# A pace, an interleaving and a first load changed in a two-block transformer kernel

## The chip, the cores and the metric

The kernel runs on one core of one Trainium2 chip. The metric is device time in microseconds (us) of one execution. Three runs of the kernel before took 1598.66, 1603.24 and 1604.40 us.

The engines are named as in the profile: PE multiplies matrices (PEld loads its stationary operand beside the products), DVE (VectorE) and ACT (ScalarE) work elementwise, POOL is GpSimd, SP only issues transfers here.

## The reference

Two blocks run one after the other on 256 tokens of width 1024, in float32. The first has two gated feed-forward layers, a mixer and an embedding gate; the second an attention block and a layer of experts that are looked up by product keys. The parts that matter here, shortened:

```python
def swiglu(x, w_gate, w_up, w_down):
    return (jax.nn.silu(x @ w_gate) * (x @ w_up)) @ w_down

h = h + 0.5 * swiglu(rms_norm(h, ln_ffn1[i]), w1_gate[i], w1_up[i], w1_down[i])
...
def peer_ffn(h, w_query, sub_keys, expert_u, expert_v):
    q = jnp.einsum('bsd,dk->bsk', h, w_query).reshape(B, S, PEER_HEADS, 2, PEER_HALF)
    sc = jnp.einsum('bshpc,hpnc->bshpn', q, sub_keys)
    s1, i1 = lax.top_k(sc[..., 0, :], PEER_TOPK)
    s2, i2 = lax.top_k(sc[..., 1, :], PEER_TOPK)
    cand_s = (s1[..., :, None] + s2[..., None, :]).reshape(...)
    cand_i = (i1[..., :, None] * N_KEYS + i2[..., None, :]).reshape(...)
    top_s, sel = lax.top_k(cand_s, PEER_TOPK)
    idx = jnp.take_along_axis(cand_i, sel, axis=-1)
    gates = jax.nn.softmax(top_s, axis=-1)
    ...
        u = expert_u[ec]
        a = jax.nn.gelu(jnp.einsum('cd,chkd->chk', xc, u), approximate=False) * wc
        return jnp.einsum('chk,chkd->cd', a, expert_v[ec])
```

There are 128 x 128 experts, 8 heads, and 16 experts for each head and token.

## The kernel before

Every float32 product is done as three: an operand is split into a high part (ACT, line 288) and a low rest (DVE, line 289), and high x low, high x high and low x high are summed (lines 314 to 324). A weight tile comes by a transfer that SP issues into a `raw` buffer; ACT makes `wh` from it and DVE `wl`; then PE uses both.

**The start.** x is loaded in four pieces (`xload(c, j)`: chunk c of 128 tokens, half j of the width). `wraw1(k, h)` loads tile k of the first weights `w1t` in h pieces. 18 products of a zero tile `z` (line 720) come first on PE. `n1.part(c, j)` transposes a piece of x on PE (line 512) and splits it into `hH` and `hL` (lines 516, 519). `cut["n"]` says in how many pieces a weight tile is split by ACT and DVE. `tm_proj` takes tile k for chunk 0 as it comes and for chunk 1 four tiles later; its `parts` say behind which tile a further piece of x is transposed.

**The expert stage (`peer`).** Instead of gathering expert rows, the kernel computes all of them. `ublock(i)` multiplies the u rows of 128 experts (first index i) with all 256 tokens: 24 products of 128x256 (lines 322 to 324) into one of four `mm` banks; gelu goes into `G[:, i, :]`. The matrix of gates comes from `wgroup(g)`, four tokens at a time: for each token PE multiplies two one-hot matrices (`B`/`BL` with `O`, lines 1615, 1616; 8 products of 128x128 a group) into an `acc` bank. DVE makes the one-hots for two groups at once in four instructions (`onehots`, lines 1601 to 1604). What exists of G for these tokens is multiplied by the gates on DVE (line 1621); where G is still to come, ACT writes the gates into G (line 1623) and a later u-block multiplies its gelu with them (lines 1634, 1635). `slotT` holds the indices and gates that the one-hots are made from. It is filled per chunk of 128 tokens by `rowcol(c)`, eight `lookup(c, half, q)` (three DVE instructions each, lines 1566, 1568, 1569) and `gates(c)` (with three transposes on PE, line 1582). Groups 0 to 31 need chunk 0, groups 32 to 63 chunk 1. After the last u-block and group, the output stage multiplies G with the v rows of each i: `operands` splits `G[:, i]` into `aH` and `aL`, and 12 products of 128x512 follow (lines 318 to 320).

**The order.** All of this background work stands in a deque `bg` with a cost for each item. After every block `run(c)` adds credit c and takes items while the credit is above 0; c is `QC` = 1.2 in the 16 query steps and `UC` = 1.0 in the 127 u-blocks after the first. What is left in `bg` is done behind the last u-block (lines 1678, 1679). A scheduler then sets the order on each engine from this program order; it may pull an instruction forward whose operands are there. Each engine takes its row in order. The deque's items for the lookup and the groups are filled in chunk by chunk:

```python
        for c in range(2):
            bg.append((1.2, lambda c=c: rowcol(c)))
            for k in range(8):
                bg.append((0.9, lambda c=c, k=k: lookup(c, *divmod(k, 4))))
            bg.append((0.8, lambda c=c: gates(c)))
            for g in range(32 * c, 32 * c + 32):
                bg.append((1.25, lambda g=g: wgroup(g)))
```

Of the kernel before, what the change touches and what calls it, by code (L numbers as in the profile page):

```python
# [13 lines left out]
OP = mybir.AluOpType  # L14
# [6 lines left out]
NEG = -1e30  # L21
FT = 4
TAIL = (5, 5)
UC = 1.0
QC = 1.2
FILL = 1200
LATE = (2, 3, 4, 5, 6, 7, 8, 9, 9, 10, 11, 12)
# [4 lines left out]
FW = 3  # L32
PR = 2
WN = 18
G2 = (0,) * 8
OKIND = ("at", "mm")
FLAG = (4, 4)
# [160 lines left out]
def _build(tc, nc, A, out, stop=99, dbg=None):  # L198
    ctx = ExitStack()
    mm_, act, dve, pool = nc.tensor.matmul, nc.scalar, nc.vector, nc.gpsimd  # L200
# [52 lines left out]
    col = const.tile([128, NCOL], F32, name="col")  # L253
# [30 lines left out]
    def ins_of(i):  # L284
        return getattr(i, "ins", i)
# [17 lines left out]
    def wsplit(raw, n=1024, p=None, g=None):  # L303
        H, L = ((p or ws[t]).tile([128, 1024], F32R, tag=t, name=t)[:, :n] for t in ("wh", "wl"))
        if gate:
            g = gate.pop()
        m = n // cut["n"]
        for i in range(0, n, m):
            if g is not None:
                pool.tensor_copy(H[:, i:i + 1], g)  # L310
            split(raw[:, i:i + m], H[:, i:i + m], L[:, i:i + m])
        return H, L
# [384 lines left out]
    n1 = RawNorm(hA, lambda dt: K("ln_ffn1", dt))  # L697
    raw1 = {}

    def wraw1(k, h=1):  # L700
        raw1[k] = ws["raw"].tile([128, 1024], F32, tag="raw", name="raw")
        m = 1024 // h
        for i in range(0, 1024, m):
            nc.sync.dma_start(raw1[k][:, i:i + m], A["w1t"][k][:, i:i + m])

    wraw1(0, 2)
    wraw1(1)
    xload(1, 0)
    wraw1(2)
    xload(0, 1)  # L710
# [4 lines left out]
    with TP("warm") as p:  # L715
# [2 lines left out]
        ps = fill_bank((128, 256))  # L718
        for _ in range(WN):
            mm_(ps, z[:, 0:128], z, start=True, stop=True)  # L720
    dve.tensor_scalar(col[:, 0:48], col[:, 0:48], 32.0, None, op0=OP.mult)
    n1.part(0, 0)
    cut["n"] = 2
    with tc.issue_after(ins_of(n1.first_act)):
        first = {0: wsplit(raw1.pop(0))}
    cut["n"] = 1
    identb = mb[:, 0:128]
    maskb = mb[:, 128:256]
# [37 lines left out]
    modp = spare.enter_context(TP("modp", 2))  # L766
    with TP("ffw1", TLW[0], side="right") as pw1:
        ffn(n1, 1, extra(FT, range(M0), NF - 1), n2, pw1, first, before_tail=ple_proj, raws=raw1,
            parts={0: (1, 0), 1: (0, 1), 2: (1, 1)})
    dump("x1", xr)  # L770
    if stop <= 1:
        pstack.close(); big.close(); early.close()
# [682 lines left out]
    def peer():  # L1455
# [87 lines left out]
        def rowcol(c):  # L1543

            slots[c] = G[:, 112:115, 128:256]
            a, w, i, j = (spare16[:, 2 + n_ // 2, n_ % 2 * 128:n_ % 2 * 128 + 128] for n_ in range(4))
            s_ = G[:, 115, 128:256].bitcast(U32)
            sf = sel[c].rearrange("p h k -> p (h k)")
            dve.tensor_scalar(s_, sf, 3, None, op0=OP.logical_shift_right)
            dve.tensor_copy(a, s_)  # L1550
            dve.tensor_scalar(s_, sf, 7, None, op0=OP.bitwise_and)
            dve.tensor_copy(w, s_)
            dve.scalar_tensor_tensor(j, a, 9.0, w, op0=OP.is_ge, op1=OP.mult)
            dve.tensor_sub(w, w, j)
            dve.tensor_scalar(i, a, -1.0, 0.0, op0=OP.add, op1=OP.max)
            dve.tensor_add(i, i, j)
            dve.tensor_scalar(j, a, 1.0, 8.0, op0=OP.is_equal, op1=OP.mult)
            dve.tensor_add(j, j, w)
            ij[c] = [x_.rearrange("p (h k) -> p h k", h=8) for x_ in (i, j)]

        def lookup(c, half_, q):

            e4 = spare16[:, 0:2].rearrange("p h (k j) -> p h k j", j=16)
            sv = ij[c][half_][:, 2 * q:2 * q + 2]
            iv = idxf[c].rearrange("p (h two) k -> p h two k", two=2)[:, 2 * q:2 * q + 2, half_]
            dve.tensor_tensor(e4, sv.unsqueeze(3).to_broadcast([128, 2, 16, 16]),
                              iob[:, 0:16].unsqueeze(1).unsqueeze(1).to_broadcast([128, 2, 16, 16]), op=OP.is_equal)
            dve.tensor_tensor(e4, e4, iv.unsqueeze(2).to_broadcast([128, 2, 16, 16]), op=OP.mult)
            dve.tensor_reduce(slots[c][:, half_, q * 32:(q + 1) * 32].rearrange("p (h k) -> p h k", h=2), e4,
                              axis=AX.X, op=OP.add)  # L1570

        def gates(c):
            g = slots[c][:, 2].rearrange("p (h k) -> p h k", h=8)
            dve.tensor_sub(g, tops[c], tops[c][:, :, 0:1].to_broadcast([128, 8, 16]))
            act.activation(g, g, AF.Exp)
            sm = ps_.tile([128, 8], F32, tag="gs", name="gs")
            dve.reduce_sum(sm, g, axis=AX.X)
            dve.reciprocal(sm, sm)
            dve.tensor_tensor(g, g, sm.unsqueeze(2).to_broadcast([128, 8, 16]), op=OP.mult)
            ps = mm_bank((128, 3, 128))  # L1580
            for i in range(3):
                nc.tensor.transpose(ps[:, i], slots[c][:, i], ident)

            sT = slotT[:, :, c * 128:(c + 1) * 128]
            two = [128, 128, 2]
            for i in range(2):
                act.activation(sT[:, i], ps[:, i].unsqueeze(2).to_broadcast(two), AF.Copy)
            act.activation(sT[:, 2], ps[:, 2].unsqueeze(2).to_broadcast(two), AF.Copy, scale=32768.0)
            dve.scalar_tensor_tensor(sT[:, 3], ps[:, 2].unsqueeze(2).to_broadcast(two), 32768.0, sT[:, 2],
                                     op0=OP.mult, op1=OP.subtract)  # L1590
# [16 lines left out]
        def wgroup(g):  # L1607
            t0 = 4 * g
            if g % 2 == 0:
                with tc.issue_after(ins_of(lasts["low"])):  # L1610
                    onehots(g // 2)
            O, H, L = (x_[:, 4 * (g % 2):4 * (g % 2) + 4] for x_ in state["oh"])
            ps = acc_bank((128, 4, 128))
            for j in range(4):
                mm_(ps[:, j], H[:, j], O[:, j], start=True, stop=False)  # L1615
                mm_(ps[:, j], L[:, j], O[:, j], start=False, stop=True)  # L1616
            cur = state["cur"]
            pv = ps.rearrange("p t i -> p i t")
            if cur > 0:
                gs = G[:, 0:cur, t0:t0 + 4]  # L1620
                dve.scalar_tensor_tensor(gs, pv[:, 0:cur], 2.0 ** -15, gs, op0=OP.mult, op1=OP.mult)
            if cur < 128:
                act.activation(G[:, cur:128, t0:t0 + 4], pv[:, cur:128], AF.Copy, scale=2.0 ** -15)
            state["td"] = t0 + 4
# [27 lines left out]
        for i in range(17):  # L1652
# [12 lines left out]
                for c in range(2):  # L1665
                    bg.append((1.4, lambda hd=nt // 2, c=c: cand(hd, c)))
            run(QC)
        for c in range(2):
            bg.append((1.2, lambda c=c: rowcol(c)))
            for k in range(8):  # L1670
                bg.append((0.9, lambda c=c, k=k: lookup(c, *divmod(k, 4))))
            bg.append((0.8, lambda c=c: gates(c)))
            for g in range(32 * c, 32 * c + 32):
                bg.append((1.25, lambda g=g: wgroup(g)))
        for i in range(1, 128):
            ublock(i)
            run(UC)
# [127 lines left out]
```

## Time and profile before

| | |
|---|---|
| three runs | 1598.66, 1603.24, 1604.40 us |
| the profiled execution, its own time | 1600.18 us |
| its span | 1598.4 us |
| PE busy | 1562.4 us, 98% |
| DVE busy | 1124.4 us, 70% |
| ACT busy | 811.6 us, 51% |
| POOL busy | 91.5 us, 6% |
| mean granted clock of PE | 0.991 |

A group of instructions is named by line, engine, operation and tile, as out<-in, with its count, its busy time, the mean of one, and the idle time of its engine ahead of it with what ended that. Products of PE overlap: one is started before the one ahead has ended, so their rate is read from the distance of their starts and not from their durations. The granted clock is 1.00 at 2.4 GHz and 0.50 at 1.2 GHz. The u-blocks run from about 770 to 1217 us, the output stage from 1233 us on.

### The profile page before, as it was taken

How to read it: one execution, taken by the hardware profiler on the slowest of the kernel's cores; microseconds unless marked ns; L12 is line 12 of the kernel's file. 1: busy time of each engine (PE TensorE's matmuls, PEld its weight loads, DVE VectorE, ACT ScalarE, POOL GpSimd, SP SyncE). 2: the span in 40 equal slices, each digit the busy share in tenths (PEclk: the TensorE clock that was granted, in tenths of full speed). 3: DMA queues.
4: the chain of work that ended last, by engine and by line, in shares of the span. 5: the costliest groups of instructions: out<-in, count | busy, mean ns of one | idle time of the engine just before them, and what ended most of it. 6: DMA issues, size and time to landing. Idle time of an engine off the chain costs nothing.

```text
span 1598.4 us, 27198 instructions
## 1 busy us (share of the span) xinstructions
PE 1562.4 (98%) x10344; PEld 1414.3 (88%) x10344; DVE 1124.4 (70%) x2205; ACT 811.6 (51%) x1553; POOL 91.5 (6%) x161
## 2 busy tenths in 40 slices
PE   9999999999999999998999999999897999999998
PEld 7999899879999789997999999999897888888886
DVE  7766768767856745557799958788888666555654
ACT  6444564564545666655554555444442445454543
POOL 1400011100000202021000000000000000000001
PEclk9999999999999999999999999999997999999999
DMA  8777754448967446431555555555453767666662
GB/s 311 238 253 250 255 165 141 120 136 300 335 211 227 152 141 204 133 119 67 187 171 185 185 176 167 160 159 177 129 164 125 234 222 230 202 187 194 214 190 92
DMA packets 84708, 299.94 MB, mean 188 GB/s; under 512 B 9600, under 2 KB 11232, under 8 KB 84192
## 3 DMA queue, kind: packets, MB, share of 16 engines
q1 hardware_dynamic: 80928, 290.92, 56.2%
q10 hardware_dynamic: 3648, 7.28, 1.3%
q8 instruction: 81, 1.33, 0.3%
q14 instruction: 51, 0.42, 0.1%
HBM read 294.95 MB, written 3.15 MB: 186 GB/s over the span
## 4 chain that ended last, share of the span: by engine, by line
PE 86%; DVE 6%; DMA 4%; ACT 2%; issue 1%; POOL 0%; SPq 0%; POOLq 0%; ACTq 0%; DVEq 0%
PE mm L322 15%; PE mm L323 14%; PE mm L324 14%; PE acc L318 11%; PE acc L320 11%; PE acc L319 11%; DVE wl L289 2%; DMA raw<-in_pv 2%; ACT wh L288 1%; DMA raw<-in_wmod 1%; PE acc L925 1%; PE acc L1615 1%; PE acc L1616 1%; PE sc L1267 1%; DMA raw<-in_wquery 1%
## 5 line engine op out<-in xcount | busy, mean ns | idle before, releaser
L289 DVE TENSOR_TENSOR wl<-raw,wh 128x1024 fp32r<-128x1024 f32 (+2 forms) x604 | 610.1, 1027 | 278.7 <-ACT wh L288 273.1
L288 ACT ACTIVATE wh<-raw 128x1024 fp32r<-128x1024 f32 (+2 forms) x604 | 527.5, 898 | 540.2 <-PE mm L323 241.3
L322 PE MATMUL mm<-hL,wh 128*128 128x256 f32 x1976 | 565.5, 286 | 4.9 <-ACT ge L1634 4.9
L324 PE MATMUL mm<-hH,wl 128*128 128x256 f32 x1976 | 560.6, 284 | 0.0
L323 PE MATMUL mm<-hH,wh 128*128 128x256 f32 x1976 | 560.3, 284 | 0.0
L322 PEld LDWEIGHTS mm<-hL,wh 128*128 128x128 f32 x1976 | 378.3, 191 | 7.9 <-ACT ge L1634 5.1
L323 PEld LDWEIGHTS mm<-hH,wh 128*128 128x128 f32 x1976 | 378.5, 192 | 2.0
L324 PEld LDWEIGHTS mm<-hH,wl 128*128 128x128 f32 x1976 | 378.2, 191 | 0.4
L318 PE MATMUL acc<-wh,aL 128*128 128x512 f32 x648 | 257.5, 397 | 2.6 <-DVE aL L289 2.6
L320 PE MATMUL acc<-wl,aH 128*128 128x512 f32 x648 | 255.5, 395 | 0.0
L319 PE MATMUL acc<-wh,aH 128*128 128x512 f32 x648 | 254.2, 392 | 0.0
L318 PEld LDWEIGHTS acc<-wh,aL 128*128 128x128 f32 x648 | 122.6, 189 | 28.9 <-issue 2.8
L320 PEld LDWEIGHTS acc<-wl,aH 128*128 128x128 f32 x648 | 122.3, 189 | 29.0 <-issue 0.2
L319 PEld LDWEIGHTS acc<-wh,aH 128*128 128x128 f32 x648 | 122.4, 189 | 27.1 <-issue 0.5
L318 PE MATMUL acc<-wh,hL 128*128 128x512 f32 x224 | 89.8, 402 | 2.8 <-DVE hL L492 1.6
L319 PE MATMUL acc<-wh,hH 128*128 128x512 f32 x224 | 88.3, 395 | 0.0
L320 PE MATMUL acc<-wl,hH 128*128 128x512 f32 (+1 forms) x224 | 86.1, 395 | 0.0
L289 DVE TENSOR_TENSOR aL<-G,aH 128x256 fp32r<-128x256 f32 x128 | 53.4, 419 | 3.1 <-ACT aH L288 3.1
L630 DVE SCALAR_TENSOR_TENSOR macc<-raw,col,macc 128x1024 f32<-128x1024 f32 x28 | 35.9, 1281 | 27.1 <-DMA raw<-in_wmod 27.0
L288 ACT ACTIVATE aH<-G 128x256 fp32r<-128x256 f32 x128 | 51.0, 401 | 5.5 <-PE acc L320 4.0
L318 PEld LDWEIGHTS acc<-wh,hL 128*128 128x128 f32 x224 | 42.8, 191 | 11.9 <-ACT wh L288 2.1
L593 ACT ACTIVATE sg<-sg 128x256 f32<-128x256 f32 x36 | 14.8, 411 | 71.6 <-DVE sg L592 66.9
(474 smaller groups left out, 1650.7 us busy)
## 6 DMA issues: line engine op xcount, KB each, us to landing
raw<-in_pu SPq DMA_DIRECT2D x128, 512.0 KB, 3.5
raw<-in_pv SPq DMA_DIRECT2D x128, 512.0 KB, 4.3
raw<-in_wmod SPq DMA_DIRECT2D x48, 512.0 KB, 4.8
raw<-in_w1gu SPq DMA_DIRECT2D x36, 512.0 KB, 4.4
raw<-in_w2gu SPq DMA_DIRECT2D x36, 512.0 KB, 4.8
raw<-in_w1d SPq DMA_DIRECT2D x22, 512.0 KB, 4.7
raw<-in_w2d SPq DMA_DIRECT2D x22, 512.0 KB, 4.3
raw<-in_wout SPq DMA_DIRECT2D x16, 512.0 KB, 3.6
```

What stands on the lines that cost most here:

```text
L288: act.activation(H, src, AF.Copy)
L289: lasts["low"] = dve.tensor_sub(L, src, H.bitcast(F32))
L318: mm_(ps, aL, bH, start=start, stop=False)
L319: mm_(ps, aH, bH, start=False, stop=False)
L320: lasts["pe"] = mm_(ps, aH, bL, start=False, stop=stop)
L322: mm_(ps, aH, bL, start=start, stop=False)
L323: mm_(ps, aH, bH, start=False, stop=False)
L324: mm_(ps, aL, bH, start=False, stop=stop)
L630: dve.scalar_tensor_tensor(macc[j], raw, K("c", k), macc[j], op0=OP.mult, op1=OP.add)
L925: mm_(ps[:, j, c], k[pr][:, j, sl], q[pr][:, j, sl], start=True, stop=True)
L1267: mm_(ps[:, o:o + n], qa[:, hd, c * 128:c * 128 + 128], ka[:, hd, 0:n], start=True, stop=False)
L1615: mm_(ps[:, j], H[:, j], O[:, j], start=True, stop=False)
```

## The change

Three things change. `UC` goes from 1.0 to 1.15. The items of the second chunk's lookup are put behind the first chunk's: rowcol and one lookup ahead of all groups, the other seven lookups and gates one by one behind every second group. At the start tile 1 of `w1t` is loaded and split in two halves like tile 0, eight more products of the zero tile stand behind the first four transposes, and the other three pieces of x are transposed one tile later each. Four lines are added ahead of the expert stage, so that line 1601 becomes 1605 and so on; line 289 becomes 290.

```diff
-UC = 1.0
+UC = 1.15
...
+WN2 = 8
...
     wraw1(0, 2)
-    wraw1(1)
+    wraw1(1, 2)
     xload(1, 0)
...
         for _ in range(WN):
             mm_(ps, z[:, 0:128], z, start=True, stop=True)
-    dve.tensor_scalar(col[:, 0:48], col[:, 0:48], 32.0, None, op0=OP.mult)
-    n1.part(0, 0)
+        dve.tensor_scalar(col[:, 0:48], col[:, 0:48], 32.0, None, op0=OP.mult)
+        n1.part(0, 0)
+        with tc.issue_after(ins_of(n1.last_pe)):
+            for _ in range(WN2):
+                mm_(ps, z[:, 0:128], z, start=True, stop=True)
     cut["n"] = 2
     with tc.issue_after(ins_of(n1.first_act)):
-        first = {0: wsplit(raw1.pop(0))}
+        first = {k: wsplit(raw1.pop(k)) for k in range(2)}
...
-            parts={0: (1, 0), 1: (0, 1), 2: (1, 1)})
+            parts={1: (1, 0), 2: (0, 1), 3: (1, 1)})
...
-        for c in range(2):
-            bg.append((1.2, lambda c=c: rowcol(c)))
-            for k in range(8):
-                bg.append((0.9, lambda c=c, k=k: lookup(c, *divmod(k, 4))))
-            bg.append((0.8, lambda c=c: gates(c)))
-            for g in range(32 * c, 32 * c + 32):
-                bg.append((1.25, lambda g=g: wgroup(g)))
+
+        looks = [[(1.2, lambda c=c: rowcol(c))]
+                 + [(0.9, lambda c=c, k=k: lookup(c, *divmod(k, 4))) for k in range(8)]
+                 + [(0.8, lambda c=c: gates(c))] for c in range(2)]
+        bg.extend(looks[0])
+        bg.extend(looks[1][:2])
+        late = deque(looks[1][2:])
+        for g in range(64):
+            bg.append((1.25, lambda g=g: wgroup(g)))
+            if g % 2 and late:
+                bg.append(late.popleft())
```

On DVE, in the lookup of the second chunk, before (`wl` is the split of a u weight, one for each u-block; `G<-G,iob`, `G<-G,idxf` and the reduce are the three of a lookup; `G<-ge,G` belongs to a u-block):

```order
L1568 TENSOR_TENSOR G<-G,idxf_8534 128x2x256
L289 TENSOR_TENSOR wl<-raw,wh 128x1024
L1569 TENSOR_REDUCE G<-G 128x32
L1635 TENSOR_TENSOR G<-ge,G 128x128
L1566 TENSOR_TENSOR G<-G,iob 128x2x256
L289 TENSOR_TENSOR wl<-raw,wh 128x1024
```

The lookups of chunk 1 now, among the one-hots `B`, `O`, `BL` and the gate products `G<-acc,G` of the first groups:

```order
L1605 TENSOR_TENSOR B<-ioh,slotT 128x1024
L1608 TENSOR_TENSOR O<-ioh,slotT 128x1024
L1570 TENSOR_TENSOR G<-G,iob 128x2x256
L1639 TENSOR_TENSOR G<-ge,G 128x16
L1625 SCALAR_TENSOR_TENSOR G<-acc,G 128x51x4
L1606 TENSOR_TENSOR BL<-B,slotT 128x1024
L1572 TENSOR_TENSOR G<-G,idxf_8545 128x2x256
L290 TENSOR_TENSOR wl<-raw,wh 128x1024
L1625 SCALAR_TENSOR_TENSOR G<-acc,G 128x52x4
L1639 TENSOR_TENSOR G<-ge,G 128x20
L1607 TENSOR_TENSOR B<-B,slotT 128x1024
L1573 TENSOR_REDUCE G<-G 128x32
```

The lookups moved from the time in which 98 u-blocks are in G to that in which some 50 are, and lie between groups. (Behind them, in the order before, the one-hots of two pairs of groups follow at once.)

On DVE, at the end of the u-blocks, before: the last one-hots and gate products, then the first weights and operands (`aL`) of the output stage:

```order
L1604 TENSOR_TENSOR O<-ioh,slotT 128x1024
L1602 TENSOR_TENSOR BL<-B,slotT 128x1024
L1621 SCALAR_TENSOR_TENSOR G<-acc,G 128x128x4 x2
L1603 TENSOR_TENSOR B<-B,slotT 128x1024
L1621 SCALAR_TENSOR_TENSOR G<-acc,G 128x128x4 x2
L289 TENSOR_TENSOR wl<-raw,wh 128x1024
L289 TENSOR_TENSOR aL<-G,aH 128x256 x4
```

The last gate product now, and what follows it:

```order
L1625 SCALAR_TENSOR_TENSOR G<-acc,G 128x119x4
L1639 TENSOR_TENSOR G<-ge,G 128x252
L290 TENSOR_TENSOR aL<-G,aH 128x256 x2
L290 TENSOR_TENSOR wl<-raw,wh 128x1024
L290 TENSOR_TENSOR aL<-G,aH 128x256
L1639 TENSOR_TENSOR G<-ge,G 128x256
L290 TENSOR_TENSOR aL<-G,aH 128x256
```

The last gate product covers 119 u-blocks in place of 128. The first four operands stand right behind it; nine u-blocks, each with its `wl` and its `G<-ge,G`, come after these, and PE's row has nine u-blocks behind its last group where it had eight groups behind its last u-block. On SP the load of the spilled x into G (line 1740) stands ahead of the last two u weights, where it stood behind seven v weights; the transfers are otherwise in the order of before, apart from the halves of tile 1.

On PE, at the start, before, from the first products of tile 0 (`wh_156`) over the transposes of x(1, 0) (`mm_189`) to those of tile 1 (`wh_202`):

```order
L319 MATMUL acc_182<-wh_156,hH_102 128x512
L320 MATMUL acc_181<-wl_157,hH_102 128x512
L320 MATMUL acc_182<-wl_157,hH_102 128x512
L512 MATMUL mm_189<-cst_88,xr_94 128x128 x4
L318 MATMUL acc_181<-wh_202,hL_103 128x512
```

The same place now, from the last of the eight products of zeros; tile 0 is `wh_165`, tile 1 `wh_171`, and x(1, 0) `mm_210`:

```order
L726 MATMUL fill_123<-z_121 128x256
L319 MATMUL acc_196<-wh_165,hL_103 128x512
L320 MATMUL acc_196<-wh_165,hH_102 128x512
L319 MATMUL acc_197<-wh_165,hL_103 128x512
L320 MATMUL acc_197<-wh_165,hH_102 128x512
L321 MATMUL acc_196<-wl_166,hH_102 128x512
L321 MATMUL acc_197<-wl_166,hH_102 128x512
L319 MATMUL acc_196<-wh_171,hL_103 128x512
L320 MATMUL acc_196<-wh_171,hH_102 128x512
L321 MATMUL acc_196<-wl_172,hH_102 128x512
```

The transposes of x(1, 0) moved from between the tiles to behind tile 1.

## Rows read from the trace of the kernel before

**Rows 1.** The page: busy time of PE, and the clock in 40 slices

```profile
PE 1562.4 (98%) x10344; PEld 1414.3 (88%) x10344; DVE 1124.4 (70%) x2205; ACT 811.6 (51%) x1553; POOL 91.5 (6%) x161
...
PEclk9999999999999999999999999999997999999999
```

**Rows 2.** Windows: length, busy PE, PEld, DVE, ACT, POOL (count), clock, DMA, GB/s

```profile
1120.00:1140.00 20.00, 14.81 (x128) 14.44 (x126) 17.67 (x30) 7.73 (x19) 0.00 (x0) 0.91 0.43 133
...
1220.00:1240.00 20.00, 12.42 (x67) 10.46 (x68) 13.38 (x23) 3.76 (x7) 0.00 (x0) 0.57 0.26 80
```

**Rows 3.** Around 1131: PE's timeline; a wait (sum, times, longest); two windows

```profile
1136.13 0.39 PE L322 MATMUL mm<-hL,wh 128*128 128x256 f32 x1 [4.92 <-ACT ge L1634]
...
ACT G L1623 <- DVE G L1621: 4.1, 4, 1.6
...
1136.00:1138.00 2.00, 1.87 (x10) 1.88 (x11) 2.00 (x5) 0.79 (x4) 0.00 (x0) 0.64 0.00 0
1138.00:1140.00 2.00, 2.00 (x12) 2.00 (x11) 1.02 (x3) 0.00 (x0) 0.00 (x0) 0.51 0.00 0
```

**Rows 4.** Groups on DVE, 884 to 945: one chunk's eight lookups

```profile
L1566 DVE TENSOR_TENSOR G<-G,iob 128x512 bf16<-128x512 bf16 x8 | 5.5, 687 | 0.1
L1569 DVE TENSOR_REDUCE G<-G 128x32 f32<-128x512 bf16 x8 | 5.5, 684 | 0.2
L1568 DVE TENSOR_TENSOR G<-G,idxf 128x512 bf16<-128x512 bf16 x8 | 3.4, 422 | 0.1
```

**Rows 5.** PE's timeline, end of the groups: start, duration, instruction, idle before

```profile
1222.66 0.29 PE L1615 MATMUL acc<-O,B 128*128 128x128 f16 x1 [4.82 <-DVE B L1603]
...
1228.83 0.29 PE L1615 MATMUL acc<-O,B 128*128 128x128 f16 x1 [2.57 <-DVE B L1603]
...
1233.06 0.77 PE L318 MATMUL acc<-wh,aL 128*128 128x512 f32 x1 [2.34 <-DVE aL L289]
...
1238.74 0.49 PE L319 MATMUL acc<-wh,aH 128*128 128x512 f32 x1
...
1239.31 0.39 PE L318 MATMUL acc<-wh,aL 128*128 128x512 f32 x1
1239.53 0.39 PE L319 MATMUL acc<-wh,aH 128*128 128x512 f32 x1
```

**Rows 6.** 1143 to 1207: the window, then PE's L322 window and DVE's groups

```profile
1143.00:1207.00 64.00, 64.00 (x597) 63.31 (x596) 55.78 (x89) 28.77 (x74) 0.00 (x0) 1.00 0.51 157
...
L322 PE MATMUL mm<-hL,wh 128*128 128x256 f32 x156 | 44.9, 288 | 0.0
...
L289 DVE TENSOR_TENSOR wl<-raw,wh 128x1024 fp32r<-128x1024 f32 x20 | 24.4, 1222 | 8.2 <-ACT wh L288 8.2
L1621 DVE SCALAR_TENSOR_TENSOR G<-acc,G 128x420 f32<-128x420 f32 (+15 forms) x16 | 10.0, 624 | 0.0
L1635 DVE TENSOR_TENSOR G<-ge,G 128x148 f32<-128x148 f32 (+16 forms) x21 | 7.0, 335 | 0.0
L1601 DVE TENSOR_TENSOR B<-ioh,slotT 128x1024 f16<-128x1024 f16 x8 | 5.5, 685 | 0.0
```

**Rows 7.** DVE's timeline where u-blocks run without groups

```profile
926.21 1.23 DVE L289 TENSOR_TENSOR wl<-raw,wh 128x1024 fp32r<-128x1024 f32 x1 [1.66 <-ACT wh L288]
929.09 1.23 DVE L289 TENSOR_TENSOR wl<-raw,wh 128x1024 fp32r<-128x1024 f32 x1 [1.66 <-ACT wh L288]
```

**Rows 8.** The timeline of the start: PE's and ACT's instructions that waited, and one behind

```profile
6.89 0.79 PE L318 MATMUL acc<-wh,hL 128*128 128x512 f32 x1 [0.97 <-ACT wh L288]
...
9.28 1.06 ACT L288 ACTIVATE wh<-raw 128x1024 fp32r<-128x1024 f32 x1 [1.67 <-DMA raw<-in_w1t]
9.95 0.72 PE L512 MATMUL mm<-cst,xr 128*128 128x128 f32 x4
10.43 0.48 PE L318 MATMUL acc<-wh,hL 128*128 128x512 f32 x1
11.23 1.06 ACT L288 ACTIVATE wh<-raw 128x1024 fp32r<-128x1024 f32 x1 [0.64 <-DMA raw<-in_w1t]
```

## The prediction, made before the change was run

> **What bounds the kernel now.** I read the page first, for the engine that fills the span: PE is busy for 1562.4 of 1598.4 us, and the granted clock shows 7 tenths in one slice of 40 [rows 1]. So the whole kernel has 36 us in which PE does nothing, and a change that leaves the number of products alone can gain only from those, or from stretches at the lower clock level. Then I read windows of the expert stage, to find where these lie: PE fills every 20 us of it except 1120 to 1140 (14.81 busy, clock 0.91) and 1220 to 1240 (12.42 busy, clock 0.57) [rows 2]. Both places are ones that the change touches: the lookup of the second chunk, and the one-hot groups left over when the u-blocks are done. Last I read the timeline, waits and groups there, for the price of each.
>
> **The lookup of the second chunk.** In the order of before its 24 lookup instructions stand on DVE alone, with no group between them; gates follow, and then the work of four groups comes in one burst. DVE then falls behind, and ACT, whose G copies wait for DVE (4.1 us in four waits), keeps the gelu that frees a mm bank waiting behind them. PE stands still for 4.92 us before 1136.13 [rows 3]. It then runs at the lower level (1.2 GHz) until about 1140: by the two windows 2 x (1 - 0.64) + 2 x (1 - 0.51) = 1.7 us are lost [rows 3]. The change spreads seven lookups and gates over the first 16 groups, so the second chunk's slots are ready some 16 groups before they are used: the burst has no cause any more. Gain 4.92 + 1.7 = **6.6 us**. What is moved costs 14.4 us of DVE for eight lookups (5.5 + 3.4 + 5.5) [rows 4], 1.8 us each; seven of them among 16 groups are 7 x 1.8 / 16 = 0.8 us a group, reckoned with the load below. No transfer belongs to a lookup; the three transposes of gates stay three transposes on PE.
>
> **The groups that were left over.** The costs in the code sum to 156 (32 halves at 1.1, 16 candidates at 1.4, two lookups at 9.2, 64 groups at 1.25), the pace gives 16 x 1.2 + 127 x 1.0 = 146; so eight groups follow the last u-block. With 1.15 it is 165, and the order of the change has nine u-blocks behind its last group. What PE loses there now: idle 4.82 (waiting for B of a one-hot), 2.57 (the same) and 2.34 (waiting for aL, the first operand of the output stage), together 9.73 us [rows 5]. Six of the eight groups ran at the lower level: four took from 1222.66 to the next wait's beginning (1228.83 - 2.57 = 1226.26), 0.90 each, where a group costs 0.49 at the full level (below), 6 x 0.41 = 2.5 us. The first 13 wide products took 5.68 us, from 1233.06 to 1238.74, 0.44 apart; at the full level they are 0.22 to 0.23 apart (1239.31 to 1239.53), 13 x 0.227 = 2.95, so 2.7 us are lost [rows 5]. Gain 9.73 + 2.5 + 2.7 = **14.9 us**. What is late next: the operands aH and aL of the first four output blocks now stand ahead of nine u-blocks on ACT and DVE, and the weights of the output stage follow those of the last u-blocks through the same buffers, as each u-block's do. I see no wait, and take 0; between 0 and 2.34, the wait that stands there now, is the bound. On SP the load of the spilled x moves ahead of the last two u weights; it waits only for those operands, which are nine blocks old by then, and adds half a megabyte to a queue whose share was 0.51 in the stretch [rows 6].
>
> **The higher pace.** DVE gets the same work in fewer blocks. A u-block with nothing else takes 929.09 - 926.21 = 2.88 us, PE's pace [rows 7]. From 1143 to 1207 there are 156 L322 products (8 a block, 19.5 blocks) and 16 groups in 64 us, all PE: (64 - 19.5 x 2.88) / 16 = 0.49 us a group. DVE there: durations sum to 24.4 + 10.0 + 7.0 + 4 x 5.5 = 63.4, busy 55.8 since neighbours overlap, a factor 0.88. Per block (24.4 + 7.0) / 20 x 0.88 = 1.38, per group (10.0 + 22.0) / 16 x 0.88 = 1.76 [rows 6]. The pace of the change is 1.15 / 1.25 = 0.92 groups a block: DVE 1.38 + 0.92 x 1.76 = 3.00 a block, PE 2.88 + 0.92 x 0.49 = 3.33. DVE stays at 90%, and at 93% where ten blocks in a row carry a group each (3.14 of 3.37). Among the first 16 groups (27.1 of cost with the lookups, 23.6 blocks, 0.68 groups a block) the lookups add 0.8 x 0.68 = 0.5 us a block: 1.38 + 0.68 x 1.76 + 0.5 = 3.1 of 3.2. Without the factor for overlap it would be 1.57 + 0.93 x 2.00 = 3.43 against 3.34, or 0.09 x 50 blocks = 4 to 5 us late in all; that is the upper bound, below it 0. I take 0.5, near 0, since DVE's only idle in the stretch, 8.2 us, is a wait for wh: it is ahead of PE, not behind.
>
> What queues behind what: a wl or a gelu's product that stands behind a one-hot waits for it. The row shows this happening: ACT's gelu stood behind a copy of G that waited for DVE, and PE waited [rows 3]. The Trainium skill, page "TensorE: Matmul & The Clock Gate", section "Architectural detail: the array is 16× 32×32, not 1× 128×128", says that ScalarE and VectorE take their queue strictly first in, first out; by that rule every one-hot pulled forward delays weights that could have gone first, which speaks against a higher pace. The trace agrees in the 4.92 us wait, and has no such wait from 1143 to 1207. The time by this rule is the second rival's.
>
> **The start.** Eight more dummy products go behind the first four transposes, w1t tile 1 comes in two halves, and each following piece of x is transposed one weight step later. PE now idles 0.97 us before its first product, is at the lower level until 9.95, and then waits for transfers: tile 1 has landed by 9.28, tile 2 by 11.23 [rows 8]; after tile 2 it never waits long. So the start can give PE little before tile 2: 0.97 of idle is filled with dummies that compute nothing, and four transposes that were done in a wait now come into the full stretch, 0.48 us (9.95 to 10.43) [rows 8]. The extra DMA issue is 0.43 us on SP in front of five loads, if it delays tile 2. The other way, products at the full level sooner could take out up to 0.5 us. Bounds -0.5 to +1.0; I take **+0.5**, the transposes.
>
> **Sum.** The profiled execution took 1600.18 us (span 1598.4). 1600.2 - 6.6 - 14.9 + 0.5 + 0.5 = 1579.7. The median of the three runs stands 3.1 us above the profiled one and the lowest run 1.5 below; I place the forecast a little under the middle of 1579.7 and 1582.8: **1581**.
>
> **Rivals.** (1) DVE becomes the bound in the groups: its 0.42 us a block of waiting (8.2 / 19.5) doesn't shrink when its work grows. Then 1.38 + 0.93 x 1.76 + 0.42 = 3.44 against PE's 3.34 over some 50 blocks, 5 us, up to 8 with the first 16 groups: 1586 to 1589. For it: DVE is already the busiest engine beside PE. Against: that wait is for buffers which PE frees, so it shrinks by itself. (2) Slower: the in-order queue lets bursts form as at 1131, each with PE idle 4.92 us and the clock down for another 1.7. It decides from the point where DVE's work exceeds PE's by more than its lead of about two blocks (6.7 us). To end over 0.5% above before it needs five such stalls, 5 x 6.6 = 33 us: 1614. Against it: pairs of blocks in the new order hold one pair of one-hots each, 6.3 us of DVE in 6.7 of PE; no row of the order has two pairs at once behind the first gates. (3) The handover keeps a gap: the operand tiles lie where the one-hots lay, and the first weights come late. 2.34 us gives 1583, and an idle near 5 us with the clock down again 5 + 2.7, 1589. (4) The change doesn't do what it says, groups still follow the last block: its order excludes that.
>
> **How the numbers follow.** Forecast 0.80 (own range 1575 to 1587), DVE the bound 0.10, a gap at the handover 0.06, bursts and slower 0.03, the rest 0.01. The range goes from 1575 (lowest run, start at its better bound, all gains) to 1590 (rivals 1 and 3) and leaves out less than 2 in 10. A measurement of this kernel tells 0.5%, 8 us, from no change. Cases 1, 3 and the forecast all end under 1595: faster 0.95; same 0.02 (several costs at once); slower 0.03.
>
> **What would show it.** Right: no 20 us window of the expert stage with PE under 19.5 busy or clock under 0.95; no wait of PE for B or a gelu over 1 us; first aH some nine blocks ahead of the first wide product, no idle before it; DVE 90 to 95% busy among the groups; first products of tile 2 at about 12.5. Wrong: PE waits for wl, B or a bank spread over the groups (rival 1), clock below 1 there (rival 2), idle at the handover (rival 3).

## The result and the profile after

Four runs of the changed kernel took 1577.72, 1579.40, 1580.44 and 1580.45 us, the median is 1579.92; the kernel before stood at 1602.41 beside it. The ratio is 0.986, with a 95% interval of 0.9841 to 0.9878. The forecast was 1581 with a range of 1575 to 1590. The profiled execution took 1577.72 us, with a span of 1575.6.

The page of the changed kernel, busy time of the engines and the clock in 40 slices:

```profile
PE 1554.0 (99%) x10352; PEld 1408.1 (89%) x10352; DVE 1122.9 (71%) x2210; ACT 812.9 (52%) x1557; POOL 91.6 (6%) x161
...
PEclk9999999999999999999999999999999999999999
```

Against [rows 1] PE has 21.6 us without work where it had 36, and the granted clock is at 9 tenths or more in every slice of 40. Windows of the changed kernel (length, busy PE, PEld, DVE, ACT, POOL, clock, DMA share, GB/s): the place of the old stall, then the last groups, the u-blocks behind them and the start of the output stage:

```profile
1120.00:1140.00 20.00, 20.00 (x192) 19.74 (x191) 18.47 (x31) 8.99 (x24) 0.00 (x0) 1.00 0.51 154
...
1180.00:1200.00 20.00, 20.00 (x177) 19.91 (x176) 13.66 (x21) 10.10 (x24) 0.00 (x0) 1.00 0.64 207
1200.00:1220.00 20.00, 20.00 (x138) 18.56 (x137) 11.56 (x15) 10.35 (x15) 0.00 (x0) 1.00 0.58 176
1220.00:1240.00 20.00, 20.00 (x89) 16.36 (x88) 12.04 (x16) 8.79 (x13) 0.00 (x0) 1.00 0.78 254
```

Both holes of [rows 2] are closed: PE is busy for all of every window from 780 to 1300 us, at the full level; in the output stage behind, it has 19.32 us from 1300 to 1320. PE's waits of the changed kernel (sum, times, longest) begin with ones of other stages; those for `B`, for a gelu and most of that for `aL` ([rows 3, 5]) are gone:

```profile
PE mm L484 <- DVE dg L454: 2.6, 1, 2.6
PE acc L319 <- DVE hL L520: 2.3, 2, 1.4
PE acc L319 <- DVE hL L493: 1.5, 1, 1.5
...
PE acc L319 <- DVE aL L290: 0.7, 1, 0.7
```

**A cleaner measure.** What lies ahead of the experts is nearly the same work in both kernels: the start lines differ, and with them the scheduler's order in the first 70 us, in a few places from 607 to 711 us and again from 755 us on. But the time of this part differs from execution to execution (last section). So I also compare the stretch from the first product of the 16 query steps (`mm<-hL,wh`) to the end of the span:

```profile
767.87 0.28 PE L322 MATMUL mm<-hL,wh 128*128 128x256 f32 x1
```

```profile
766.75 0.28 PE L323 MATMUL mm<-hL,wh 128*128 128x256 f32 x1
```

The first row is of the kernel before, the second of the changed one: 1598.4 - 767.87 = 830.5 and 1575.6 - 766.75 = 808.9, so 21.7 us are gained there and 1.1 ahead of it. The 21.7 close: 6.6 for the stall, 9.73 + 2.5 + 2.7 for the end of the groups, 0.9 because PE waited 1.7 us for the scores' operands before (0.4 and 1.3) and 0.9 after (0.2 and 0.7), less a wait of 0.7 for `aL` in the output stage that is new.

The wait for the scores' operands is longer with the old start and shorter with the new one, though the start lies 770 us ahead: the longest wait for `qT` on ACT is 1.2 to 1.7 us in the five profiles with the old start and 0.7 in all nine with the new one. The scheduler, given another start, set another order here too: with the old start PE does one round of scores ahead of this wait, with the new one three. The kernel before, then the changed one:

```profile
776.41 0.71 PE L1508 MATMUL mm<-G,qT 128*128 128x128 f32 x4 [1.31 <-ACT qT L1500]
```

```profile
775.89 0.71 PE L1512 MATMUL mm<-G,qT 128*128 128x128 f32 x4 [0.68 <-ACT qT L1504]
```

The stretch has a spread of its own as well: kernels with the pace and the lookup of the change stand at 808.9, 811.3 (no_start) and 810.8 (no_warm), partly by waits for `aL` in the output stage of 0.7, 1.6 and 1.9 us. Differences below some 2.5 us are therefore not read from one profile each.

### The profile page after: what moved, and what is told of

It is laid out like the page before. It is cut to its first block, busy times and chain, and to the rows that moved or that the text cites. A ratio compares the mean times of both kernels' runs of the same rounds, so it can differ in the third digit from the quotient of the medians.

```text
span 1575.6 us, 27238 instructions
## 1 busy us (share of the span) xinstructions
PE 1554.0 (99%) x10352; PEld 1408.1 (89%) x10352; DVE 1122.9 (71%) x2210; ACT 812.9 (52%) x1557; POOL 91.6 (6%) x161
## 4 chain that ended last, share of the span: by engine, by line
PE 89%; DMA 5%; DVE 3%; ACT 2%; issue 1%; POOL 0%; SPq 0%; POOLq 0%; ACTq 0%; DVEq 0%
PE mm L323 15%; PE mm L324 15%; PE mm L325 15%; PE acc L319 12%; PE acc L321 11%; PE acc L320 11%; DMA raw<-in_pv 2%; DMA raw<-in_wmod 2%; ACT wh L289 1%; DVE wl L290 1%; PE acc L1619 1%; PE acc L1620 1%; PE acc L929 1%; PE sc L1271 1%; PE mm L1512 0%
## 5 line engine op out<-in xcount | busy, mean ns | idle before, releaser
L289 ACT ACTIVATE wh<-raw 128x1024 fp32r<-128x1024 f32 (+3 forms) x605 | 528.0, 897 | 539.2 <-PE mm L324 251.7
L290 DVE TENSOR_TENSOR wl<-raw,wh 128x1024 fp32r<-128x1024 f32 (+3 forms) x605 | 610.8, 1026 | 266.0 <-ACT wh L289 262.7
L594 ACT ACTIVATE sg<-sg 128x256 f32<-128x256 f32 x36 | 14.9, 413 | 69.8 <-DVE sg L593 66.5
```

The lines of the kernel that those rows point to most:

```text
L289: act.activation(H, src, AF.Copy)
L290: lasts["low"] = dve.tensor_sub(L, src, H.bitcast(F32))
```

## The experiments

All in one table; "stretch" is the measure above (span less the start of the first query product). Ratios are to the kernel before beside it, whose median was 1601 to 1603.

| kernel | median us | ratio, interval | stretch us |
|---|---|---|---|
| before | 1602.41 | | 830.5 |
| changed | 1579.92 | 0.986, 0.9841 to 0.9878 | 808.9 |
| pace_only | 1587.25 | 0.9924, 0.9907 to 0.994 | 816.3 |
| weave_only | 1593.03 | 0.9956, 0.9939 to 0.9974 | 823.8 |
| start_only | 1599.32 | 0.9989, 0.9977 to 1.0001 | 829.1 |
| no_start | 1581.41 | 0.9884, 0.9868 to 0.9901 | 811.3 |
| pace_108 | 1579.57 | 0.9859, 0.9825 to 0.9892 | 810.2 |
| pace_130 | 1579.04 | 0.9852, 0.9824 to 0.988 | 809.2 |
| pace_150 | 1588.73 | 0.9909, 0.9875 to 0.9942 | 820.4 |
| pace_180 | 1604.75 | 1.001, 0.9994 to 1.0026 | 833.3 |
| burst4 | 1577.71 | 0.9852, 0.9816 to 0.9889 | 809.8 |
| early_all | 1581.22 | 0.9871, 0.9843 to 0.9899 | 808.6 |
| pace_spacer | 1581.68 | 0.9868, 0.9839 to 0.9898 | 812.2 |
| no_warm (one run) | 1579.79 | | 810.8 |

**The parts alone.** pace_only is the kernel before with one number changed:

```diff
-UC = 1.0
+UC = 1.15
```

> Only UC = 1.15; lookup and start as before. Theory (two separate holes): the gap at the end of the groups goes (14.9 us), the stall after the second chunk's lookup stays (6.6 us), so about 1602.4 - 14.9 = 1587.5 us (1585 to 1590), with PE idle for 3 to 6 us behind the second chunk's gates and the clock below 1 there. Rival 1 (the pace alone does it all, the stall was one of too little lead): 1581 us and no such idle. Rival 2 (a higher pace makes the burst denser): the stall at least doubles, 1594 us or more.

Measured: 1587.25 us, as the theory of two separate holes has it. The stall is still there, in a stretch that carries the second chunk's gates; two waits of its PE timeline, and the window around:

```profile
1092.94 0.39 PE L322 MATMUL mm<-hL,wh 128*128 128x256 f32 x1 [1.94 <-DVE slotT L1589]
...
1100.95 0.39 PE L322 MATMUL mm<-hL,wh 128*128 128x256 f32 x1 [3.08 <-ACT ge L1634]
...
1090.00:1110.00 20.00, 14.98 (x144) 14.52 (x143) 18.48 (x34) 6.34 (x16) 0.00 (x0) 0.91 0.30 99
```

1.94 + 3.08 = 5.0 us idle, and by the mean clock of 0.91 some 20 x 0.09 = 1.8 us more: about the price of [rows 3] again, in another order. Neither rival fits.

weave_only has the reordered lookup and nothing else:

```diff
+        bg.extend(looks[0])
+        bg.extend(looks[1][:2])
+        late = deque(looks[1][2:])
...
+            if g % 2 and late:
+                bg.append(late.popleft())
```

> Only the second chunk's lookup is woven between the first groups; UC = 1.0 and the start as before. Theory: the stall near 1131 us goes, the eight groups behind the last u-block stay with their three waits (9.7 us) and the lower clock, so about 1602.4 - 6.6 = 1595.8 us (1594 to 1598). Rival (the burst comes from the gates and the four groups behind them, not from where the lookup stands): the idle of 4 to 5 us stays somewhere among the groups, about 1602 us.

Measured: 1593.03 us, a little under the expected range; the stretch is 6.8 us shorter than before, where 6.6 were due. Its PE waits for `B` and `aL` are those of [rows 5]:

```profile
PE acc L1615 <- DVE B L1603: 7.4, 2, 4.8
...
PE acc L318 <- DVE aL L289: 2.3, 1, 2.3
```

The two parts give 14.2 and 6.8 us of stretch, 21.0 together. Both in one kernel give 19.2 with the old start (no_start) and 21.7 with the new: they add, as far as the spread of the stretch lets one tell.

start_only (the start's lines of the change, `UC = 1.0` and the old order) and no_start (the other way about):

> Only the change of the start; pace and lookup as before. By the prediction's term 0.5 us later, by the trace of the changed kernel 0.4 us earlier (the DVE instruction r<-n,r began at 57.12 before and 56.70 after): no difference in time can be seen, 1602 us, 1600 to 1604. In the trace that DVE instruction at 56.7 if the gain is the start's own, at 57.1 if it was chance; the first products 0.23 to 0.25 us apart in place of 0.43.

> The change without its start: UC = 1.15 and the woven lookup, the start as before. Theory: 0.4 us above the changed kernel, 1580.3 us (1578 to 1583), all the gain is in the expert stage. Rival (the start gives 2 us, as the trace of after stands 2.0 us ahead at 571 us): 1582 us, and 571 us for the block that is at 569.3 in the changed kernel.

Measured: 1599.32, a little under the expected range, with an interval that reaches no change, and 1581.41. The instruction that was to decide, `r<-n,r`, does not: it begins at 56.19 in start_only, but with the old start at 56.47 in no_start and 56.65 in pace_only, so 57.12 was late in that one execution. Further on, the residual of the second feed-forward layer (`xr<-acc,rh`, on DVE) begins at 519.06 before and 518.66 after, but at 518.76, 518.66 and 518.69 in pace_only, weave_only and no_start, which all have the old start, and at 518.61 in start_only. So nothing of the start arrives there; the 0.4 us by which I had it ahead were the one execution. What the start lines do change is the order of the query steps (above): the wait of 0.7 in place of 1.2 to 1.7 us. The medians point the same way, by 1.9 us (start_only against the kernel before) and 1.5 us (no_start against the changed one), but not clear of noise. no_start also refutes the rival of 2 us: it is at 571 us as early as the changed kernel (569.3 both).

no_warm takes the eight further products of zeros out (`WN2 = 0`):

> The changed kernel without the eight further products of zeros. Theory (tile 2 of the first weights ends the waits of the start, whatever PE did before): the products of tile 0 run 0.43 us apart at the lower level, but the instruction on DVE that ends the first feed-forward layer's residual (xr<-acc,rh, near 518.7 us) begins within 0.2 us of the changed kernel's. Rival (the dummies bring the start forward): 0.5 to 1.0 us later there.

One run took 1579.79 us. The instruction begins at 518.76, 0.1 from the changed kernel's. (It belongs to the second feed-forward layer; the first one's begins at 191.08, against 191.01.) But the other half of the expectation was wrong: without the dummies the products of tile 0 were not slow either.

```profile
6.61 0.50 PE L319 MATMUL acc<-wh,hL 128*128 128x512 f32 x1 [1.69 <-ACT wh L289]
6.95 0.40 PE L320 MATMUL acc<-wh,hH 128*128 128x512 f32 x1
7.26 0.50 PE L319 MATMUL acc<-wh,hL 128*128 128x512 f32 x1
7.60 0.39 PE L320 MATMUL acc<-wh,hH 128*128 128x512 f32 x1
```

They start 0.31 to 0.34 us apart, behind a wait of 1.69 us; 0.43 was the distance in the profiled execution before, 0.23 to 0.31 in the changed kernel. The other four profiles with the old start (pace_only, weave_only, no_start, pace_spacer) have 0.23 to 0.34 as well, without the eight products. So these products run fast without the dummies, too, and the slow ones of [rows 8] were that one execution. The granted clock does not help here: it reads 1.00 in this place in the kernel before, too, so the lower level that the prediction spoke of at the start rests on the distances only.

**How much pace DVE bears.** The changed kernel with `UC = 1.08`, 1.3, 1.5 and 1.8.

> The changed kernel with UC = 1.08, so that the last group stands with the last u-block and no block is left over to cover the first operands of the output stage. Theory (the nine blocks behind the groups are what covers the handover): a wait for aL of about 2.3 us at the first wide product, with 0 to 2.7 us more at the lower clock: 1582 to 1585 us. Rival (any pace that leaves no group over is enough): 1580 us and no wait at the first wide product.

> The changed kernel with UC = 1.3: 1.04 groups a block, DVE 3.21 of 3.39 us a block by the prediction's sums, 95%, and 69.5 of 67.8 us over the first 16 groups with lookups. By the load alone 0 to 2 us above the changed kernel: 1580 to 1582. By the rule of 5.8 us between two splits: the densest place in the order holds some 6.4 us, so one wait of up to 3 us, 1580 to 1584. Rival (the load of DVE limits from 95% on): 1585 and more, with waits all along the groups.

> The changed kernel with UC = 1.5: 1.2 groups a block, DVE 1.38 + 1.2 x 1.76 = 3.49 us a block against 3.47 of PE, just at the limit; the first 16 groups with lookups 65.6 against 59.7. Theory: 0 to 7 us above the changed kernel, 1580 to 1587 us, DVE at 98% or more and the waits, if any, in the first 16 groups. Rival (it is bursts and not the mean load): 1590 us and more, since pairs of one-hots now stand two in a row in the order.

> The changed kernel with UC = 1.8. Theory (DVE's load decides from 100% on): 1.44 groups a block, DVE 1.38 + 1.44 x 1.76 = 3.91 us a block against 3.59 of PE; the 48 later groups take 33 blocks, 0.32 x 33 = 11 us late; the first 16 with the lookups some 15 blocks, DVE 61.5 against 51 us, 10 us late; less a lead of two blocks, 6.7 us. So 14 to 21 us above the changed kernel: 1594 to 1601 us, with DVE at 97% or more and PE waits of 1 us and more spread over the groups. Rival (DVE's waits for wh shrink as it is loaded and its instructions overlap more): 1580 to 1585 us.

1.08, 1.15 and 1.3 cannot be told apart. With 1.08 one u-block is left behind the last group, and the first wide product waits 0.48 us, where I had expected 2.3 and more:

```profile
1214.04 0.50 PE L319 MATMUL acc<-wh,aL 128*128 128x512 f32 x1 [0.48 <-DVE aL L290]
```

So nine blocks of cover are not needed; that no group is left over is what counts. 1.3 brought no wait among the groups: neither the load rival nor the one wait by the rule of 5.8 us came.

At 1.5 and 1.8 time is lost: 1588.73 us lies between what theory and rival had said, 1604.75 above both. It is not lost evenly over the groups, as a DVE that is full would do it. The long waits of PE (pace_150, then three of pace_180) lie where the lookups stand, one of them ahead of the first group (925.92 us in pace_180) and the others among the first groups:

```profile
931.58 0.23 PE L1619 MATMUL acc<-O,B 128*128 128x128 f16 x1 [2.07 <-DVE B L1607]
938.88 0.58 PE L323 MATMUL mm<-hL,wh 128*128 128x256 f32 x1 [5.34 <-ACT ge L1638]
```

```profile
903.40 0.45 PE L1586 MATMUL mm<-cst,G 128*128 128x128 f32 x1 [9.02 <-DVE G L1573]
...
932.90 0.58 PE L323 MATMUL mm<-hL,wh 128*128 128x256 f32 x1 [5.02 <-ACT ge L1638]
...
972.25 0.39 PE L323 MATMUL mm<-hL,wh 128*128 128x256 f32 x1 [2.05 <-ACT ge L1638]
```

Behind them the pace itself does little harm. pace_150 in a window among the later groups, and pace_180 in one:

```profile
1080.00:1100.00 20.00, 20.00 (x193) 19.83 (x192) 19.43 (x33) 9.67 (x26) 0.00 (x0) 1.00 0.45 144
```

```profile
1060.00:1080.00 20.00, 19.10 (x192) 18.76 (x191) 19.46 (x36) 9.47 (x22) 0.00 (x0) 1.00 0.33 110
```

With DVE at 97% PE loses nothing in the one and 0.9 us in the other; from 1040 to 1120 us pace_180 has four such waits, 2.2 us together. pace_180's total, 24.5 us of stretch above the changed kernel, exceeds the 14 to 21 of the theory, and its largest single piece is of another kind: the transposes of gates (L1586) stand in PE's row ahead of u-block products whose operands are there, and wait 9.02 us for the lookups. A high pace costs by what it puts ahead of what in a row.

**What made the stall.** Was it four groups at once? burst4 takes the second chunk's groups four at a time, at the same mean pace:

```diff
+        for g in range(32, 64, 4):
+            bg.append((5.0, lambda g=g: [wgroup(g + j) for j in range(4)]))
```

> The changed kernel with the 32 groups of the second chunk taken four at a time at the same mean pace (cost 5.0 for four); the load of DVE over the stretch is the same. Theory of bursts (four groups are 7.0 us of DVE, more than two blocks of lead): half or more of the eight bursts make PE wait, 2 to 5 us each, with the clock down after them: 1595 to 1620 us. Rival (only the mean load counts, the stall of before came from the lookup and gates ahead of the four groups): 1580 us, no wait of PE over 1 us among the groups.

Measured: 1577.71 us, with no wait of PE among the groups. My theory fell that four groups at once in the program make PE wait. It is no test of a burst on DVE, though: the scheduler put the one-hots of these groups ahead, among several blocks, so that between two splits of a weight DVE has at most 5.1 us of other work, where it has 9.7 in the kernel before. DVE does four gate products in a row, 1.87 us together, and in ACT's row two of the copies stand ahead of the next gelu (L1638) and two behind it. One row of DVE's timeline, then three of ACT's:

```profile
1091.37 1.87 DVE L1625 SCALAR_TENSOR_TENSOR G<-acc,G 128x360 f32<-128x360 f32 x4 [0.43 <-PE acc L1620]
```

```profile
1092.38 0.30 ACT L1627 ACTIVATE G<-acc 128x152 f32<-128x152 f32 x1
...
1094.33 0.30 ACT L1638 ACTIVATE ge<-mm 128x160 f32<-128x160 f32 x1
1094.51 0.49 ACT L1627 ACTIVATE G<-acc 128x152 f32<-128x152 f32 x2
```

In the kernel before the same products lie apart, each with a one-hot behind it, and ACT's row has the four copies of G (L1623) ahead of the gelu (L1634) that frees PE's bank. DVE's timeline, then ACT's, of the kernel before, ahead of the wait in [rows 3]:

```profile
1131.13 0.56 DVE L1621 SCALAR_TENSOR_TENSOR G<-acc,G 128x392 f32<-128x392 f32 x1
1131.61 0.68 DVE L1601 TENSOR_TENSOR B<-ioh,slotT 128x1024 f16<-128x1024 f16 x1
1132.21 0.56 DVE L1621 SCALAR_TENSOR_TENSOR G<-acc,G 128x400 f32<-128x400 f32 x1
1132.69 0.68 DVE L1604 TENSOR_TENSOR O<-ioh,slotT 128x1024 f16<-128x1024 f16 x1
```

```profile
1132.81 0.26 ACT L1623 ACTIVATE G<-acc 128x112 f32<-128x112 f32 x1 [0.81 <-DVE G L1621]
1133.89 0.26 ACT L1623 ACTIVATE G<-acc 128x108 f32<-128x108 f32 x1 [0.82 <-DVE G L1621]
1134.98 0.26 ACT L1623 ACTIVATE G<-acc 128x104 f32<-128x104 f32 x1 [0.83 <-DVE G L1621]
1135.79 0.49 ACT L1634 ACTIVATE ge<-mm 128x136 f32<-128x136 f32 x2 [0.55 <-DVE G L1635]
```

The copies start 1.08 us apart, where burst4's gate products need 1.87 / 4 = 0.47 each, and the gelu comes after all four: two in-order rows that hold each other up. DVE is busy without a break meanwhile (2.00 of every 2 us from 1130 to 1138). The stalls of pace_150 and pace_180 have the same pattern: four copies ahead of the gelu, 0.8 us apart, with a one-hot behind each gate product.

Is the weaving needed, or only that the slots are early? early_all puts all eight lookups and the gates of the second chunk ahead of the first group:

```diff
-        bg.extend(looks[1][:2])
-        late = deque(looks[1][2:])
+        bg.extend(looks[1])
+        late = deque()
```

> The changed kernel with all eight lookups and the gates of the second chunk ahead of the first group, none woven between groups. Theory (what counts is that slots are there long before the groups that use them, so that no two pairs of one-hots stand between two weight splits): no wait of PE among the groups, 1580 us (1578 to 1583). Rival (the weaving itself is needed, since it evens DVE's load): sixteen lookups in a row make DVE late, a wait of 2 us or more before the first groups, 1583 us or more.

Measured: 1581.22, stretch 808.6, no wait among the groups. The weaving is not needed; that the slots are early is enough.

pace_spacer keeps the lookup where it was (with `UC = 1.15`) and lets the groups behind it come later:

```diff
             bg.append((0.8, lambda c=c: gates(c)))
+            if c:
+                bg.append((4.0, lambda: None))
```

> The kernel before with UC = 1.15 and, behind the second chunk's gates, an empty item of cost 4.0, so that its first groups come three to four blocks later; the lookup stays where it was. In the order two pairs of one-hots and four gate products (about 7.0 us of DVE) still stand between two weight splits, but with four splits in a row ahead of them. Theory (a stall needs more than two blocks, 5.8 us, of other DVE work between two splits; 9.4 us in the kernel before, 8.2 in the one with the pace alone, at most 5.8 where PE did not wait): a shorter stall, 1 to 4 us, 1582 to 1587. Rival (the stall comes from groups that are due before their slots are there): none, 1580 to 1581.

Measured: 1581.68, a little under the range of the theory and above the rival's, with one wait, 2.27 us, and no lower clock behind it. So three to four blocks between the slots and their groups shorten the stall and do not end it:

```profile
1106.82 0.39 PE L322 MATMUL mm<-hL,wh 128*128 128x256 f32 x1 [2.27 <-ACT ge L1634]
```

The DVE durations between two weight splits (`wl`) rank these waits, but set no sharp limit: 9.7 us before (wait 4.9; the expectation had 9.4), 8.2 in pace_only (3.1), 6.8 in pace_spacer (2.3), 13.6 in pace_150 (5.3), 12.1 in pace_180 (5.0); at most 3.7 in the changed kernel, 4.5 in pace_130, 5.1 in burst4, all without a wait. pace_180 breaks the rank both ways: 6.7 us at 946 without a wait, and 2.05 us of wait at 972 with no more than 3.6 there. So the work that gathers on DVE and the order of ACT's row remain as causes of the stall side by side. No run changes one without the other, and how the two weigh is open.

## Why the prediction was right, step by step

- **What bounds it.** Right: PE's gaps and its lower level were all there was to gain. One window was overlooked: before, PE is busy for 17.85 of the 20 us from 1200 to 1220, too, but that is the beginning of the 4.82 us wait, and is in the sum. The profiled execution came to 1577.72 for a sum of 1579.7; in the stretch from the query steps on, the terms 6.6 + 14.9 - 0.5 = 21.0 stand against 21.7 measured. That they agree to 0.7 is partly luck: 0.9 of the 21.7 came at the query steps, where nothing was forecast, and the spread of the stretch is above 2 us. Of the signs named, one window fell short, 19.32 us busy from 1300 to 1320, by the new wait of 0.7 us for `aL`.
- **The second chunk's lookup, 6.6 us.** Right in size (6.8 in weave_only) and in that it goes. Of the reason, one part is shown: with the second chunk's slots early the stall goes (weave_only, early_all). Four groups at once in the program are harmless in burst4, where their one-hots come ahead. The rows of the stall show one-hots between the gate products and ACT's gelu behind all the copies; which of the two it takes is not shown. The spreading over 16 groups is not needed (early_all).
- **The groups left over, 14.9 us.** Right: 14.2 by the pace alone. The first `aH` comes at 1188.65 us, the first wide product at 1211.98, eight blocks of 2.88 later (nine were forecast), and nothing waits:

```profile
1188.65 0.71 ACT L289 ACTIVATE aH<-G 128x256 fp32r<-128x256 f32 x2
...
1211.98 0.39 PE L319 MATMUL acc<-wh,aL 128*128 128x512 f32 x1
```

- **What is late next, 0 taken of 0 to 2.34.** Right, and even without the cover only 0.48 (pace_108).
- **The higher pace, 0.5 us.** Nothing was lost. DVE is busy for 155.78 of 180 us from 1000 to 1180, 87%, where 90 were forecast. The forecast share was too high since I took the gate product's 624 ns from the last stretch, [rows 6]; over the 180 us it is 526, as it grows with the blocks that are in G:

```profile
L1625 DVE SCALAR_TENSOR_TENSOR G<-acc,G 128x256 f32<-128x256 f32 (+47 forms) x48 | 25.2, 526 | 0.0
...
1000.00:1180.00 180.00, 180.00 (x1690) 177.93 (x1689) 155.78 (x256) 85.88 (x216) 0.00 (x0) 1.00 0.51 158
```

- **The start, +0.5 us.** Mis-sized, inside its bounds: 0 at the start itself by the runs. The step that failed is that the four transposes come into a full stretch. They stand ahead of tile 2 at 11.46 us, and PE's next product then starts when ACT has made tile 2's `wh`:

```profile
11.46 0.60 PE L513 MATMUL mm<-cst,xr 128*128 128x128 f32 x4
12.03 0.50 PE L319 MATMUL acc<-wh,hL 128*128 128x512 f32 x1
...
10.91 1.07 ACT L289 ACTIVATE wh<-raw 128x1024 fp32r<-128x1024 f32 x1 [0.60 <-DMA raw<-in_w1t]
```

They are still hidden behind the transfer, and in the other profiles with the new start PE waits for that `wh` another 0.3 to 0.9 us behind them; 12.5 was forecast for that product. The dummies do not fill the idle either: the first product of tile 0 comes at 6.88 us, with 0.94 of idle ahead of it, where it was 6.89 and 0.97. What the new start is worth came in a place that the prediction did not name, the order of the query steps.
- **The rivals.** DVE as the bound: its 5 to 8 us don't show at 1.15, nor at 1.3. Its premise, that DVE's waits for `wh` don't shrink from 0.42 us a block, fell: 3.5 us over 12 splits, 0.3 a block, in the changed kernel's last groups, 1143 to 1181:

```profile
L290 DVE TENSOR_TENSOR wl<-raw,wh 128x1024 fp32r<-128x1024 f32 x12 | 14.7, 1221 | 3.5 <-ACT wh L289 3.5
```

Bursts that cost 6.6 each: not in this order, but such stalls are real, since pace_150 and pace_180 have them at 5.3 and 5.0 us, and at 1.8 they eat the whole gain together with the 9.02 us of the transposes. On row order the prediction cited the Trainium skill, page "TensorE: Matmul & The Clock Gate", section "Architectural detail: the array is 16× 32×32, not 1× 128×128": ScalarE and VectorE take their queues strictly first in, first out. The rows on DVE and ACT above agree with it (copies 1.08 us apart, the gelu last).

## What to carry to other kernels

Work that an engine off the bound does in the background must be over before the stage ends: a few groups left over cost 14 us here, most of it as waits and a lower clock around them, and a pace 8% higher was enough. When such work makes the bound engine wait, look at the rows of the engines between: in the stall, copies stood ahead of a gelu, each waiting for a product that had other work in front of it, while DVE had 9.7 us of such work in one place. The engine's mean load did not decide: in stretches of 20 us it reached 97% with 0 to 0.9 us lost. The cure that the runs show is to have the inputs of such work ready long before it is due.

## What the runs showed that I had not expected

**The same instructions, another clock.** Between the start and the query steps all these kernels do the same work, with about the same idle of PE in the place shown, but not at the same clock. Windows of the kernel before (first two) and of the changed kernel (next two) around 560 us, then the same two kernels around 754 us:

```profile
556.00:560.00 4.00, 1.86 (x11) 1.45 (x11) 3.77 (x10) 4.00 (x12) 0.00 (x0) 0.96 0.62 220
560.00:564.00 4.00, 4.00 (x12) 3.13 (x12) 1.42 (x6) 3.08 (x12) 1.62 (x4) 0.61 0.00 0
```

```profile
556.00:560.00 4.00, 1.93 (x9) 1.55 (x10) 3.58 (x10) 4.00 (x13) 0.04 (x1) 1.00 0.50 179
560.00:564.00 4.00, 4.00 (x19) 3.27 (x19) 1.48 (x6) 2.68 (x10) 1.87 (x5) 1.00 0.00 0
```

```profile
752.00:756.00 4.00, 3.15 (x25) 2.96 (x26) 3.54 (x13) 3.17 (x11) 1.26 (x3) 1.00 0.65 266
```

```profile
752.00:756.00 4.00, 4.00 (x24) 4.00 (x23) 3.85 (x13) 3.62 (x11) 0.69 (x3) 0.63 0.42 168
```

About 2 us without work stand ahead of 560 in both; the clock falls to 0.61 in the one and stays at 1.00 in the other. Of the fourteen profiles six fell there (0.57 to 0.67: before, pace_only, weave_only, pace_108, early_all, pace_spacer), with either start; four others at 754 (0.57 to 0.67 in their windows: changed, start_only, no_warm, and pace_180 from 754 to 758), all with the new start. What decides I do not know. Such a dip is worth some 1.5 us (4 x 0.39, 4 x 0.37).

**A drift ahead of the experts.** In pace_130 a product waits 1.99 us near 192 us for an operand; weights there (`raw<-in_w1d`) could be taken up by ACT 1.6 us later than in the changed kernel (176.88 against 175.27), which has no such wait. It is not one late transfer: ACT runs 1.2 us behind already at 145 us. pace_180 has such a wait too, 2.56 us at 192.97. What makes the drift is open.

```profile
192.08 0.50 PE L319 MATMUL acc<-wh,aL 128*128 128x512 f32 x1 [1.99 <-DVE aL L290]
```

Its query steps begin at 769.53, against 765.72 in pace_150. So the part that the pace does not touch varies by 4 us from profile to profile; the stretch behind it varies less, by some 2.5 us.
